# Hybrid attention block on one core: swapping the last two products of the output projection, and spreading the weight sums over a head

## The chip, the cores and the metric

One core of a Trainium2 chip. The metric is the device time of one execution in microseconds, the median of several runs. A profiled execution gives the rows shown below.

## The reference, cut to what matters

512 tokens, width 2048. An input projection gives queries, keys, values and gates for eight stick-breaking heads and latents for eight MLA heads; both attentions give 128 columns a head, which are gated and set side by side as `mixed` (512 x 2048).

```python
mixed = concat([o_a * silu(sb_gate), o_b * silu(mla_gate)], axis=-1)
y = mixed @ w_out                                   # 2048 x 2048
return x + rms_norm(y, post_norm_w)                 # a norm over each row of y
```

The norm needs the sum of squares of a whole row of y before any of the row can be written out.

## The kernel before

Every float32 operand is cut in two parts (`split`: a cast on ScalarE, ACT, gives `hi`; a subtraction on VectorE, DVE, gives `lo`), and each product is three matmuls (`mm3`, L127): hi·hi, hi·lo, lo·hi.

**Order.** A planner writes each engine's instruction list: among instructions whose inputs it reckons ready, the earlier in the program goes first. `tc.keep_in_program_order` pins an instruction behind the one traced just before it on the same engine. All matmuls are pinned, so TensorE (PE) runs in the order of the program; so are SyncE's (SP) loads, the weight sums on DVE (L476) and their loads and stores on GpSimd's (POOL's) DMA queue (L468, L477). Other DVE, ACT and POOL instructions may move. Each engine then runs its list strictly in order.

**Filler.** `filler` yields after each small group of matmuls of the projections; `fill(n)` takes n such steps. The attention heads put them between their own steps, so PE has dense work while DVE and ACT work on a head.

**Stick-breaking heads** (the loop at L924, h = 0 to 7). For each of four query blocks b: scores `z` on PE, mask on DVE (L936), two sigmoids on ACT, a scan on DVE (L940), and the product into `beta` (L942). Then for j = 0 to 3: transposes `tp` on PE, their split `th` (ACT) and `tl` (DVE), and `av` matmuls that read `th` and `tl`.

**Output projection.** `out_group(0)` and `(1)` make y's first 1024 columns directly. The last 1024 columns go by Strassen-Winograd on 2 x 2 blocks, seven products instead of eight (`last_columns`): x = A11·B11; then z = S1·T1, y = S2·T2, v = S3·T3, v += A22·T4, x += A12·B21 and S4·B22. S are sums of blocks of `mixed`, T sums of blocks of w_out. In the code `w11`, `w21`, `w22` are B11, B21, B22. Six products stream their weights (`product`, L563). The weights of the seventh, S4·B22, are loaded and split ahead (`keep_weights`, 16 tiles `woh`, `wol`), so that it can run row block by row block: row block 0 whole, row block 1 in two slices of 256 columns, each in a PSUM bank of its own (`sp`).

`out_piece` (L411) closes a piece of y straight from PSUM: ACT squares and sums it, DVE multiplies by the norm's weight. `sum_piece` (L419) has a sum first: DVE adds a tile, ACT squares, DVE multiplies. `residual` (L618) adds the squares, takes the power on POOL (L625, L626), and multiplies and adds x on DVE (L634), with one piece of the last row block on ACT and POOL (L631, L632).

**Weight sums.** T is made during the stick-breaking heads in eight portions. `load_weight_parts(j)` loads four tiles of 256 KB (`wsum`) on POOL's queue; `weight_sums(j)` makes four DVE subtractions of 128x512, each followed by a store to DRAM (`w_sums`). `w_todo` gives portion j to head j for j = 0 to 6, and portion 7 to head 4 too. The tiles have tag `qrt`, with eight slots; the first four tile pairs of `split_mixed` (L381: load `mx` from DRAM on POOL's queue, split to `mxh`, `mxl`) take `qrt` slots after them. The loads `mx` have tag `mv`, with four slots.

Of the kernel before, what the change touches and what calls it, by code (L numbers as in the profile page):

```python
# [2 lines left out]

# [17 lines left out]
S = 512  # L21
# [3 lines left out]
H = 8  # L25
# [32 lines left out]
def block(ctx: ExitStack, tc: tile.TileContext, a: dict):  # L58
# [16 lines left out]
    def zbank(name, dt=F32):  # L75
        return psum.tile([P, S], dt, tag="z", name=name, bufs=2)
# [10 lines left out]
    def load(out, in_):  # L87
        tc.keep_in_program_order(nc.sync.dma_start(out=out, in_=in_))
# [38 lines left out]
    def mm3(out, sth, stl, mvh, mvl, first, last, **kw):  # L127
        mm(out, sth, mvh, first, False, **kw)
        mm(out, sth, mvl, False, False, **kw)
        mm(out, stl, mvh, False, last, **kw)  # L130
# [280 lines left out]
    def out_piece(b, at, ps, pw, junk=None):  # L411

        w = ps.shape[1]
        square_sum(b, ps, (zbank("junk") if junk is None else junk)[:, :w])
        y = g(f"y{b}", tag=next(y_tags))[:, :w]
        dve.tensor_tensor(out=y, in0=ps, in1=pw, op=ALU.mult)  # L416
        ypw[b][at] = y
# [53 lines left out]
    def weight_sums(j):  # L471

        i, c = j // 2, slice((j % 2) * S, (j % 2 + 1) * S)
        b11, b12, b22, b21 = w_parts.pop(j)
        for n, (out, x, y) in ((0, (b11, b12, b11)), (2, (b12, b22, b12)), (1, (b22, b22, b11)), (3, (b21, b21, b22))):
            tc.keep_in_program_order(dve.tensor_tensor(out=out, in0=x, in1=y, op=ALU.subtract))  # L476
            tc.keep_in_program_order(pool.dma_start(out=w_sums[n][i][:, c], in_=out))  # L477

    def mixed_again(n):
        t = g("mx", tag="mv")  # L480
# [35 lines left out]
    def keep_weights():  # L516

        def loaded(j):
            t = g("wk", tag="mv")
            load(out=t, in_=a["w_o"][3, 4 + j // 2][:, (j % 2) * S:(j % 2 + 1) * S])  # L520
            return t

        raws = [loaded(0), loaded(1)]
        yield
        for j in range(8):
            if j + 2 < 8:
                raws.append(loaded(j + 2))
            hi, lo = g("woh", F32R), g("wol", F32R)
            split(hi, lo, raws.pop(0))
            kept.append((hi, lo))  # L530
            yield
# [3 lines left out]
    def load_x(b0, tag):  # L535

        for b in (b0, b0 + 1):
            x_rows[b] = []
            for i in range(4):
                xr = g("xr", tag=tag)  # L540
                load(out=xr, in_=a["x"][b * P:(b + 1) * P, i * S:(i + 1) * S])
                x_rows[b].append(xr)
                if i % 2:
                    yield
# [18 lines left out]
    def product(banks, which, srcs, start, stop, beside=iter(())):  # L563
        for i in range(4):
            wh, wl = weights(srcs[i], 1024)
            next(beside, None)
            for j in (2 * i, 2 * i + 1):
                s_ = slice((j % 2) * S, (j % 2 + 1) * S)
                for r in range(2):
                    mm3(banks[r], *factor(which, j, r), wh[:, s_], wl[:, s_], start and j == 0, stop and j == 7,  # L570
                        skip_group_check=True)
                    yield

    def last_columns():
        w11, w21 = ([a["w_o"][2, k + i] for i in range(4)] for k in (0, 4))
        x = [bank("sx") for _ in range(2)]
        sums_of = late_sums()
        yield from product(x, "A11", w11, True, False, sums_of)
        s1 = [g("s1", tag="t") for _ in range(2)]
        s15 = [g("s15", tag="t") for _ in range(2)]  # L580
        for r in range(2):
            act.copy(out=s1[r], in_=x[r])
        z = [zbank("sz") for _ in range(2)]
        yield from product(z, "S1", w_sums[0], True, True, sums_of)
        for r in range(2):
            dve.tensor_tensor(out=s15[r], in0=z[r], in1=s1[r], op=ALU.add)
        y = [tbank("sy") for _ in range(2)]
        keeping = keep_weights()
        yield from product(y, "S2", w_sums[1], True, True)
        next(keeping)  # L590
        for r in range(2):
            dve.tensor_tensor(out=s1[r], in0=y[r], in1=s1[r], op=ALU.add)
            dve.tensor_tensor(out=s15[r], in0=y[r], in1=s15[r], op=ALU.add)
        pw2, pw3 = post_weight(2), post_weight(3)
        junk = g("junk", tag="tr")
        v = [bank("sv") for _ in range(2)]
        yield from product(v, "S3", w_sums[2], True, False, keeping)
        for r in range(2):
            sum_piece(2 + r, 3 * S, v[r], s15[r], pw3, junk)
        yield from product(v, "A22", w_sums[3], False, True, both(keeping, load_x(2, "g")))  # L600
        for r in range(2):
            sum_piece(2 + r, 2 * S, v[r], s1[r], pw2, junk)
        yield from product(x, "A12", w21, False, True, load_x(0, "qrt"))
        for r in range(2):
            out_piece(r, 2 * S, x[r], pw2, junk)
        for b in (2, 3):
            residual(b)
        for b in (0, 1):
            cuts = [slice(0, S)] if b == 0 else [slice(0, 256), slice(256, S)]
            for s_ in cuts:  # L610
                ps = zbank("sp")[:, :s_.stop - s_.start]
                for j in range(8):
                    mm3(ps, *factor("S4", j, b), kept[j][0][:, s_], kept[j][1][:, s_], j == 0, j == 7)
                    yield
                sum_piece(b, 3 * S + s_.start, ps, s15[b][:, s_], pw3[:, s_], junk)
            residual(b, b == 1)

    def residual(b, tail=False):  # L618
        xs = x_rows[b]
        n = pieces[b]  # L620
        part = tn("part")
        dve.tensor_reduce(out=part, in_=ssy[b][:, :n - 1], axis=AX.X, op=ALU.add)
        dve.tensor_scalar(out=part, in0=part, scalar1=EPS, scalar2=None, op0=ALU.add)
        r2 = tn("r2")
        pool.tensor_tensor(out=r2, in0=ssy[b][:, n - 1:n], in1=part, op=ALU.add)  # L625
        pool.tensor_tensor(out=r2, in0=r2, in1=mhalf[:, :1], op=ALU.pow)  # L626
        for i, (at, y) in enumerate(sorted(ypw[b].items())):
            w = y.shape[1]
            o = xs[at // S][:, at % S:at % S + w]
            if tail and i == 2:  # L630
                act.activation(out=y, in_=y, func=AF.Copy, scale=r2)  # L631
                pool.tensor_tensor(out=o, in0=y, in1=o, op=ALU.add)  # L632
            else:
                dve.scalar_tensor_tensor(out=o, in0=y, scalar=r2, in1=o, op0=ALU.mult, op1=ALU.add)  # L634
            (nc.sync, nc.scalar)[i % 2].dma_start(out=a["out"][b * P:(b + 1) * P, at:at + w], in_=o)
# [285 lines left out]

    w_todo = [[h] for h in range(H - 1)] + [[]]
    w_todo[H // 2].append(H - 1)
    for h in range(H):  # L924
        kh, kl = need("k", h)
        qh, ql = need("q", h)
        fill(4)
        rows = row_tiles("beta")
        for j in w_todo[h]:
            load_weight_parts(j)  # L930
        for b in range(NB):
            n = (b + 1) * P
            w = max(n, 256)
            z = zbank("z")
            mm3(z[:, :w], tokens(qh, b), tokens(ql, b), kh[:, :w], kl[:, :w], True, True)
            dve.tensor_tensor(out=z[:, n - P:n], in0=z[:, n - P:n], in1=m_sb, op=ALU.add)  # L936
            keep, prod, beta = g("keep", tag="tr"), g("prod", tag="tr"), rows[b]
            act.activation(out=keep[:, :n], in_=z[:, :n], func=AF.Sigmoid, scale=rq_neg[:, b:b + 1])
            act.activation(out=beta, in_=z[:, :n], func=AF.Sigmoid, scale=rq_pos[:, b:b + 1])
            dve.tensor_tensor_scan(out=prod[:, :n][:, ::-1], data0=keep[:, :n][:, ::-1], data1=zero.broadcast_to([P, n]),  # L940
                                   initial=1.0, op0=ALU.mult, op1=ALU.add)
            dve.tensor_tensor(out=beta[:, :n - 1], in0=beta[:, :n - 1], in1=prod[:, 1:n], op=ALU.mult)  # L942
            fill((1, 3, 3, 7)[b])
        for j in w_todo[h]:
            weight_sums(j)
        cur = Weighted(rows, need("v", h // 4), (h % 4) * P)
        for j in range(NB):
            cur.turn(j)
            fill(3)
            cur.add(j)  # L950
        out = cur.finish(need("gate", h))
        if h == H - 1:
            last_mixed[0] = out
        put_aside(h, out)
# [58 lines left out]
```

## Time and profile before

| | |
|---|---|
| median of 3 runs | 852.98 us (851.91 to 856.62) |
| profiled execution, its time | 854.35 us |
| its span, first to last instruction | 852.6 us |
| PE matmul busy | 834.7 us, 98% |
| DVE busy | 484.3 us, 57% |
| ACT busy | 361.7 us, 42% |
| granted TensorE clock, mean | 0.996 |

The profile's rows are times in microseconds from the span's start. PE is busy nearly throughout, so what counts is the few places at which it waits, and the stretch after its last matmul.

### The profile page before, as it was taken

The numbers are of one execution on the slowest core, as the hardware profiler recorded it, in microseconds if no ns is written. First come the engines' busy times: TensorE is split into PE (matmuls) and PEld (weight loads), VectorE is DVE, ScalarE is ACT, GpSimd is POOL, SyncE is SP. The second block draws the span as 40 slices with busy tenths as digits, with TensorE's granted clock in tenths as the row PEclk, the third lists the DMA queues.
The fourth block names the chain that finished last, engine by engine and source line by source line (L and its number), as shares of the span: only waits on it lengthen the run. The fifth ranks groups of instructions, "written<-read, shape, count | busy, mean of one in ns | idle before, by whom it ended". The sixth has DMA issues, their size and how long they took to land.

```text
span 852.6 us, 11037 instructions
## 1 busy us (share of the span) xinstructions
PE 834.7 (98%) x4074; PEld 701.4 (82%) x4074; DVE 484.3 (57%) x869; ACT 361.7 (42%) x622; POOL 90.7 (11%) x189
## 2 busy tenths in 40 slices
PE   8999999999999999999999999999999999999995
PEld 5889988888888888888888888888878887888784
DVE  5576765565665523647374523566473777435875
ACT  6742655545555323334242413333352644334531
POOL 1000000000000020111111020121120121100001
PEclk9999999999999999999999999999999999999998
DMA  9923322222221153434434352345463555526874
GB/s 329 345 81 106 100 81 81 81 93 81 81 88 67 63 185 99 149 107 153 161 124 161 123 200 94 142 145 187 149 210 111 161 196 200 161 98 212 321 282 148
DMA packets 42053, 126.84 MB, mean 149 GB/s; under 512 B 5824, under 2 KB 6352, under 8 KB 42000
## 3 DMA queue, kind: packets, MB, share of 16 engines
q1 hardware_dynamic: 30096, 88.75, 30.0%
q0 software_dynamic: 10608, 35.42, 12.3%
q10 hardware_dynamic: 1296, 1.97, 0.7%
q8 instruction: 32, 0.52, 0.2%
q14 instruction: 21, 0.17, 0.1%
HBM read 109.34 MB, written 16.78 MB: 148 GB/s over the span
## 4 chain that ended last, share of the span: by engine, by line
PE 86%; DVE 4%; DMA 4%; issue 3%; ACT 2%; POOL 1%; SPq 0%; DVEq 0%; POOLq 0%; ACTq 0%
PE gps L122 19%; PE v L122 10%; PE qp L122 10%; PE kp L122 9%; PE y L122 6%; PE cq L122 4%; PE av L122 4%; PE mz L122 3%; DMA mx<-mixed 3%; PE mqp L122 3%; PE sx L122 3%; PE ckv L122 2%; PE tp L125 2%; PE sv L122 2%; PE z L122 2%
## 5 line engine op out<-in xcount | busy, mean ns | idle before, releaser
L99 DVE TENSOR_TENSOR wlo<-raw,whi 128x1024 fp32r<-128x1024 f32 (+2 forms) x137 | 163.3, 1192 | 147.7 <-ACT whi L96 144.1
L96 ACT CAST whi<-raw 128x1024 fp32r<-128x1024 f32 (+2 forms) x137 | 140.4, 1026 | 216.0 <-PE v L122 43.5
L122 PE MATMUL gps<-hh,whi 128*128 128x512 f32 x256 | 102.0, 398 | 0.0
L122 PE MATMUL gps<-hl,whi 128*128 128x512 f32 x256 | 100.1, 391 | 0.0
L122 PE MATMUL gps<-hh,wlo 128*128 128x512 f32 x256 | 99.9, 390 | 0.0
L122 PEld LDWEIGHTS gps<-hh,wlo 128*128 128x128 f32 x256 | 48.0, 188 | 10.6
L99 DVE TENSOR_TENSOR tl<-tp,th 128x512 fp32r<-128x512 f32 (+1 forms) x64 | 31.2, 487 | 42.5 <-ACT th L96 42.0
L96 ACT CAST th<-tp 128x512 fp32r<-128x512 f32 (+1 forms) x64 | 27.2, 424 | 66.2 <-PE tp L125 66.0
L122 PEld LDWEIGHTS gps<-hl,whi 128*128 128x128 f32 x256 | 48.3, 189 | 7.6
L122 PEld LDWEIGHTS gps<-hh,whi 128*128 128x128 f32 x256 | 48.2, 188 | 7.6
L122 PE MATMUL qp<-hh,whi 128*128 128x512 f32 x128 | 52.1, 407 | 0.0
L122 PE MATMUL v<-whi,hh 128*128 128x512 f32 x128 | 50.9, 397 | 0.0
L122 PE MATMUL y<-whi,mxh 128*128 128x512 f32 x128 | 50.3, 393 | 0.4 <-DVE y L416 0.4
L122 PE MATMUL qp<-hh,wlo 128*128 128x512 f32 x128 | 50.1, 391 | 0.0
L122 PE MATMUL qp<-hl,whi 128*128 128x512 f32 x128 | 50.0, 391 | 0.0
L122 PE MATMUL v<-whi,hl 128*128 128x512 f32 x128 | 49.9, 390 | 0.0
L122 PE MATMUL v<-wlo,hh 128*128 128x512 f32 x128 | 49.9, 390 | 0.0
L122 PE MATMUL y<-whi,mxl 128*128 128x512 f32 x128 | 49.9, 390 | 0.0
L122 PE MATMUL y<-wlo,mxh 128*128 128x512 f32 x128 | 49.8, 389 | 0.0
L122 PE MATMUL kp<-hh,whi 128*128 128x512 f32 x128 | 49.8, 389 | 0.0
L122 PE MATMUL kp<-hl,whi 128*128 128x512 f32 x128 | 49.8, 389 | 0.0
L122 PE MATMUL kp<-hh,wlo 128*128 128x512 f32 x128 | 49.8, 389 | 0.0
(290 smaller groups left out, 1798.2 us busy)
## 6 DMA issues: line engine op xcount, KB each, us to landing
raw<-in_w_t SPq DMA_DIRECT2D x64, 512.0 KB, 3.3
raw<-in_w_o SPq DMA_DIRECT2D x24, 512.0 KB, 3.3
mx<-mixed POOLq DMA_DIRECT2D x39, 256.0 KB, 3.4
raw<-in_w_v SPq DMA_DIRECT2D x16, 512.0 KB, 3.2
wsum<-in_w_o POOLq DMA_DIRECT2D x32, 256.0 KB, 5.5
w_sums<-wsum POOLq DMA_DIRECT2D x32, 256.0 KB, 2.7
raw<-w_sums SPq DMA_DIRECT2D x16, 512.0 KB, 3.5
xs<-in_x SPq DMA_DIRECT2D x16, 256.0 KB, 6.2
```

Source lines behind the costliest of these rows:

```text
L96: i = act.copy(out=hi, in_=src)
L99: dve.tensor_tensor(out=lo, in0=src, in1=hi.bitcast(F32), op=ALU.subtract)
L122: tc.keep_in_program_order(pe.matmul(out=out, lhsT=lhsT, rhs=rhs, start=start, stop=stop, **kw))
L125: tc.keep_in_program_order(pe.transpose(out, in_, identity))
```

## The change

1. The last two products change places. S4·B22 streams its weights from `w22` into two banks `z` and is closed by `sum_piece`; A12·B21 goes last, with kept weights, and adds onto x in x's own banks: row block 0 whole, then row block 1 in two column slices of the same bank, each closed by `out_piece`.
2. `weight_sums` becomes a generator: one sum and one store per step. A step is taken behind `beta` of each block b and behind each `av` of j.
3. The parts for head h + 1 are loaded in head h, ahead of `finish`; those for head 0 ahead of the loop.
4. In the last row block, ACT and POOL take the piece of index 4 (columns 1536 to 2047) in place of index 2 (columns 1024 to 1535): with the new slices these are the ones of 512 columns.

```diff
@@ weight_sums
             tc.keep_in_program_order(pool.dma_start(out=w_sums[n][i][:, c], in_=out))
+            yield
@@ keep_weights
-            load(out=t, in_=a["w_o"][3, 4 + j // 2][:, (j % 2) * S:(j % 2 + 1) * S])
+            load(out=t, in_=a["w_o"][2, 4 + j // 2][:, (j % 2) * S:(j % 2 + 1) * S])
@@ last_columns
-        w11, w21 = ([a["w_o"][2, k + i] for i in range(4)] for k in (0, 4))
+        w11, w22 = ([a["w_o"][gi, k + i] for i in range(4)] for gi, k in ((2, 0), (3, 4)))
...
-        yield from product(x, "A12", w21, False, True, load_x(0, "qrt"))
+        z = [zbank("sz") for _ in range(2)]
+        yield from product(z, "S4", w22, True, True, load_x(0, "qrt"))
         for r in range(2):
-            out_piece(r, 2 * S, x[r], pw2, junk)
+            sum_piece(r, 3 * S, z[r], s15[r], pw3, junk)
...
-                ps = zbank("sp")[:, :s_.stop - s_.start]
                 for j in range(8):
-                    mm3(ps, *factor("S4", j, b), kept[j][0][:, s_], kept[j][1][:, s_], j == 0, j == 7)
+                    mm3(x[b][:, s_], *factor("A12", j, b), kept[j][0][:, s_], kept[j][1][:, s_], False, j == 7, skip_group_check=True)
                     yield
-                sum_piece(b, 3 * S + s_.start, ps, s15[b][:, s_], pw3[:, s_], junk)
+                out_piece(b, 2 * S + s_.start, x[b][:, s_], pw2[:, s_], junk)
@@ residual
-            if tail and i == 2:
+            if tail and i == 4:
@@ loop over the stick-breaking heads
+    load_weight_parts(0)
     for h in range(H):
...
-        for j in w_todo[h]:
-            load_weight_parts(j)
+        w_steps = itertools.chain(*(weight_sums(j) for j in w_todo[h]))
         for b in range(NB):
...
+            next(w_steps, None)
             fill((1, 3, 3, 7)[b])
-        for j in w_todo[h]:
-            weight_sums(j)
...
             cur.add(j)
+            next(w_steps, None)
+        if h < H - 1:
+            for j in w_todo[h + 1]:
+                load_weight_parts(j)
         out = cur.finish(need("gate", h))
```

## Rows read from the trace of the kernel before

**Rows 1.** The page's busy times (share of the span, instructions).

```profile
PE 834.7 (98%) x4074; PEld 701.4 (82%) x4074; DVE 484.3 (57%) x869; ACT 361.7 (42%) x622; POOL 90.7 (11%) x189
```

**Rows 2.** Busy time by stretch: us; engines with instructions; clock; DMA share; GB/s.

```profile
401.30:439.10 37.80, 37.80 (x180) 31.62 (x179) 21.08 (x33) 13.35 (x22) 5.29 (x11) 1.00 0.41 146
596.00:633.80 37.80, 36.33 (x170) 29.90 (x170) 22.79 (x37) 16.19 (x27) 8.57 (x17) 1.00 0.50 171
```

**Rows 3.** PE's waits, 600 to 680: waited for, us in total, times, longest.

```profile
PE z L122 <- ACT kh L96: 1.1, 1, 1.1
PE z L122 <- DVE kl L99: 0.3, 1, 0.3
PE av L122 <- DVE tl L99: 0.3, 1, 0.3
```

**Rows 4.** The chain that ended last: start, us, what (`y`: out_group's first matmuls).

```profile
401.32 2.04 PE qp L122 x9
439.10 2.04 PE qp L122 x9
...
595.98 2.04 PE qp L122 x9
...
674.13 2.04 PE y L122 x9
```

**Rows 5.** ACT's timeline: start, us, instruction [idle before, releaser].

```profile
624.23 0.62 ACT L96 CAST mxh<-mx 128x512 fp32r<-128x512 f32 x1 [2.29 <-DMA mx<-mixed]
624.76 0.61 ACT L96 CAST kh<-kr 128x512 fp32r<-128x512 f32 x1
```

**Rows 6.** POOL's timeline around the loads for head 6.

```profile
604.25 0.20 POOL L778 MEMSET tl<- 128x128 f32 x1
...
610.87 0.55 POOL L468 DMA_DIRECT2D wsum<-in_w_o  x1
...
613.62 1.15 POOL L392 DMA_DIRECT2D mx<-mixed  x2
621.39 1.17 POOL L392 DMA_DIRECT2D mx<-mixed  x2 [6.62 <-DVE mxl L99]
```

**Rows 7.** DVE's timeline in an undisturbed head (h = 2).

```profile
431.74 0.68 DVE L476 TENSOR_TENSOR wsum<-wsum 128x512 f32<-128x512 f32 x1
...
439.58 0.69 DVE L942 TENSOR_TENSOR beta<-beta,prod 128x511 f32<-128x511 f32 x1
...
442.52 0.68 DVE L99 TENSOR_TENSOR tl<-tp,th 128x512 fp32r<-128x512 f32 x1
```

**Rows 8.** PE's timeline in the same head.

```profile
440.98 0.60 PE L125 MATMUL tp<-ident,beta 128*128 128x128 f32 x4
...
443.71 0.39 PE L122 MATMUL av<-tl,vh 128*128 128x512 f32 x1
```

**Rows 9.** DVE's timeline at the end.

```profile
834.39 0.69 DVE L416 TENSOR_TENSOR y<-sx,pw 128x512 f32<-128x512 f32 x1 [0.34 <-ACT junk L407]
...
839.79 2.74 DVE L634 SCALAR_TENSOR_TENSOR xr<-y,r,xr 128x512 f32<-128x512 f32 x4 [0.70 <-POOL r L626]
842.45 0.75 DVE L423 TENSOR_TENSOR y<-sp,s 128x256 f32<-128x256 f32 x2
...
845.26 3.21 DVE L634 SCALAR_TENSOR_TENSOR xr<-y,r,xr 128x512 f32<-128x512 f32 x4 [0.70 <-POOL r L626]
```

**Rows 10.** ACT's timeline at the end.

```profile
838.18 0.19 ACT L407 ACTIVATION_READ_ACCUMULATOR junk<-y 128x1 f32 x1
...
843.00 0.42 ACT L407 ACTIVATE junk<-y 128x256 f32<-128x256 f32 x1 [4.63 <-DVE y L423]
843.33 0.18 ACT L407 ACTIVATION_READ_ACCUMULATOR junk<-y 128x1 f32 x1
```

**Rows 11.** PE's timeline: second and last of the 48 matmuls on two slices.

```profile
836.77 0.28 PE L122 MATMUL sp<-wol,s 128*128 128x256 f32 x1
...
842.29 0.28 PE L122 MATMUL sp<-woh,s 128*128 128x256 f32 x1
```

More of the change, by code (lines that the diff above doesn't have):

```diff
@@ L1 @@
+import itertools
 import math
```

## The prediction

> **What bounds the kernel now.** I read the page's busy times first: PE is busy for 834.7 us [rows 1], so the time is the matmuls' own unless PE waits. Then the busy times by stretch, head by head: an undisturbed stick-breaking head has PE busy for all of its 37.80 us, at full clock, while DVE has 21.08 us of work in it. The stretch from 596 to 633.8 is the exception: 36.33 us busy [rows 2]. The list of PE's waits names what it waited for there: 1.1 us for the cast `kh`, 0.3 us for `kl`, 0.3 us for `tl` [rows 3]. What this costs is read better from the chain that ended last, since a busy PE also counts the pipelined ends of its matmuls. From the first `qp` of one head to that of the next it is 439.10 - 401.32 = 37.78 us. The two heads from 595.98 to 674.13 took 78.15 us, and 2 x 37.78 = 75.56: so 2.6 us were lost in head 6 [rows 4].
>
> Why is `kh` late? ACT ran it at 624.76, right behind a cast `mxh` that began at 624.23 after 2.29 us of waiting for the load `mx` [rows 5]. ACT runs in order, so `kh` stood in line behind a cast for the output projection that is needed much later. That load left POOL's queue at 621.39, once an earlier `mxl` had freed a tile; the loads of that pair had left at 613.62, behind the weight parts of head 6, which went from 610.87 on [rows 6].
>
> The other place is the end. After PE's last matmul (842.29 + 0.28 = 842.57 [rows 11]) come add, square, power and the last multiply-adds, which begin at 845.26 [rows 9]. Nothing covers that.
>
> **The change part by part.** *Matmuls.* S4·B22 and A12·B21 have 48 matmuls of 512 columns each when streamed, and as many matmuls and slices when kept as before. SP's loads keep number, size and order; the tiles kept ahead come from another group of w_out. PE's work: 0, hidden by nothing because nothing is added.
>
> *Loads of the weight parts, one head earlier.* The four loads for head 6 are pinned behind POOL's last instruction ahead of them. That was the store of the head's output; now it is the memset of `tl`, at 604.25 against 610.87 for the first load before: some 6.4 us earlier [rows 6]. The pairs `mxh`, `mxl` that take `qrt` slots come after them, and the loads `mx` follow: those of 613.62 and 621.39 should move to about 607 and 615, and the cast that blocked ACT from 624.23 to about 618. Then `kh` has ACT to itself at 624. What is queued behind the moved loads on POOL is the store of the head's output, up to eight issues of 0.55 us [rows 6] later in head 3, four elsewhere; it is read again only by `mx` loads, later on. Gain: between 0 (another cast slips in ahead of `kh`) and 2.6 us. I take 2.6, as the shift is longer than the 2.29 us that ACT waited [rows 5].
>
> *Weight sums between the blocks.* The same 32 subtractions and 32 stores. Before, they were free to run ahead of the scores (one at 431.74 [rows 7]); now each is pinned behind the `beta` of its block. The first three lie in front of later blocks, where DVE pauses while ACT computes sigmoids. The fourth must come after the last `beta` (439.58 + 0.69 = 440.27) and so stands ahead of the split `tl`, which ended at 442.52 + 0.68 = 443.20 [rows 7]. PE reads it at 443.71 [rows 8]: 0.51 us of cover. A sum takes 0.68 us [rows 7], so each head may lose 0.68 - 0.51 = 0.17 us; in seven heads 1.2 us. Below, 0: the planner puts it behind `tl`. Above, the third sum too delays the last chain: 2 x 0.68 - 0.51 = 0.85 us, in seven heads 6.0 us. I take 1.2: if one sum makes the last `beta` late, that is covered, since 440.27 is 0.71 us ahead of the transposes at 440.98 [rows 7, 8]. The second portion's sums of head 4 come behind `av`, where DVE has the 16 us that a head leaves it [rows 2]. A store now waits for its own sum on POOL's queue; behind it there is the memset of the j = 3 transposes, some us later. Nothing.
>
> *The end, without a new wait.* `out_piece` has no add ahead of its square. PE ends at 842.57; the square of 256 columns takes 843.33 + 0.18 - 843.00 = 0.51 us [rows 10]; from a square's end to the first multiply-add it is 839.79 - (838.18 + 0.19) = 1.42 us [rows 9, 10]. So 842.57 + 0.51 + 1.42 = 844.5 in place of 845.26: 0.75 us gained. The multiplication by the norm's weight lies beside the power on POOL.
>
> *The end, with one.* Before, each slice of row block 1 had its bank. Now both lie in one bank of x. The trace shows what happens to two engines on one bank: DVE's multiplication of x, which needs nothing from ACT's square of x, stood 0.34 us idle until that square was done [rows 9]. They only read, and were put one behind the other. If this holds between a matmul and a reader of other columns, the second slice's matmuls must wait for square and multiplication of the first. [...]
>
> The price: a matmul on a slice takes (842.29 - 836.77) / 46 = 0.12 us [rows 11]. The first slice ends at about 839.7, its square at 840.2. Its multiplication then stands on DVE behind the four multiply-adds of row block 0. Those began at 839.79 [rows 9], and without the add (0.7 to 0.8 us) they begin at about 839.0 and end, 2.74 us later [rows 9], at 841.75. Before, the adds of the slices ran at 842.45, behind all four, though the first was ready by 839.8 [rows 9]: the same order is to be expected. Multiplication until 842.15, then 24 x 0.12 = 2.9 us and 0.16 us of drain to 845.2, square to 845.7, and 1.42 us to 847.1. That is 1.85 us later than 845.26. Were the multiplication put ahead of the last multiply-adds, it would be 840.2 + 0.4 + 3.05 + 0.51 + 1.42 = 845.6, 0.3 us later. Range of this term: -0.75 to +1.85. I take 1.85, the case nearest to the rows 9.
>
> *Index 4 in place of 2.* One piece of 512 columns for another, on the same engines: 0.
>
> **Sum:** -2.6 + 1.2 + 1.85 = +0.45 us. The profiled execution took 854.35 us with a span of 852.6; it lies 1.4 us above the median of 852.98, so the sum is put on the median: 853.4 us.
>
> **The rivals.**
> - *No wait at the bank.* Matmuls and readers on other columns of a bank run side by side. For it: columns are apart, and no row shows a matmul held so. Against: the readers in rows 9. -2.6 + 1.2 - 0.75 = -2.15: 850.8 us.
> - *The loss in head 6 stays,* so that the move does not do what it could. The planner may put other `mxh` casts in front of `kh`, for their loads still take turns at four slots. 0 + 1.2 + 1.85 = +3.05: 856.0 us, 0.36% more.
> - *The sums hold the heads up: slower.* Third and fourth sum both lie on the way from the last scores to `tl`: 6.0 us in place of 1.2. For it: each is pinned behind a `beta` and earlier in the program than what follows. Against: DVE idles in this stretch. -2.6 + 6.0 + 1.85 = +5.25: 858.2 us. It passes 0.5% from 0.72 us a head on.
>
> **How the numbers follow.** A measurement of this kernel can tell about 0.5% (4.3 us) from no change. Forecast 0.45, no wait at the bank 0.22, loss stays 0.20, sums hold up 0.10, the rest 0.03. No case reaches 4.3 us of gain: with all three terms at their best it is 2.6 + 0 + 0.75 = 3.35 us, so faster gets 0.06, for what I do not see and for scatter. Slower gets the last rival and the upper edge of the third case, 0.14; the same 0.80. The range from 850.0 to 857.5 takes in the first three cases with about 1 us beyond them, and leaves out the last.
>
> **What would show it.** Head 6 right: its loads `wsum` leave POOL behind the memset near 604, no wait of PE for `kh`, and 75.6 us for the two heads. Sums right: PE waits for `tl` by 0.1 to 0.2 us in each head, DVE with one `wsum` between `beta` and `tl`. The end right: PE idle for some 2.5 us between the slices of row block 1, released by DVE's multiplication. The prediction is wrong if PE waits at transposes in each head, or if its last 48 matmuls run on without a gap.

## The result and the profile after

The changed kernel takes 860.53 us (median of 6, 859.11 to 864.02), the kernel before 852.67 in the same rounds: a ratio of 1.009, interval 1.0064 to 1.0116. It is slower by 0.9%, outside the predicted range, and close to the rival that had a chance of 0.10. The profiled execution has a span of 859.6 us, 7.0 more than before.

Line numbers are now one or two higher: the sums are L477, `beta` L944, `mm3`'s matmuls L123.

PE's waits in the whole span (waited for, us in total, times, longest), to be held against [rows 3]:

```profile
PE av L123 <- DVE tl L100: 3.5, 6, 0.6
PE sx L123 <- DVE y L417: 2.0, 1, 2.0
...
PE tp L126 <- DVE beta L944: 1.1, 1, 1.1
```

Before, `tl` was waited for once; now once in six of the seven heads that take sums (in the seventh, head 3, PE waits 0.9 us for `gt` behind it in the same list). The wait for `kh` is gone. A new wait of 2.0 us stands at the end, for DVE's multiplication of x (L417).

The chain that ended last shows what a head costs (start, us, what; `gps` x15 opens heads 2 and 3):

```profile
427.70 3.40 PE gps L123 x15
...
466.74 3.40 PE gps L123 x15
```

39.04 us a head, where [rows 4] had 37.78: 1.26 us lost in a head that lost nothing before. From the first gate matmul of head 0 to the first `y` matmul of the output projection it is 330.6 us, against 323.5 before: 7.1 us. That is about the difference in the span; the rest nearly cancels (1.0 us more at the end, about as much less at the start and in the output projection together).

Why `tl` is late is on DVE's list. Its timeline in head 2, the head of [rows 7]:

```profile
435.54 0.69 DVE L477 TENSOR_TENSOR wsum<-wsum 128x512 f32<-128x512 f32 x1
436.14 0.29 DVE L938 TENSOR_TENSOR z<-z,m_sb 128x128 f32<-128x128 f32 x1
436.34 1.22 DVE L100 TENSOR_TENSOR wlo<-raw,whi 128x1024 fp32r<-128x1024 f32 x1
437.47 0.95 DVE L942 TENSOR_TENSOR_SCAN prod<-keep,zero 128x384 f32<-128x384 f32 x1
438.53 0.56 DVE L944 TENSOR_TENSOR beta<-beta,prod 128x383 f32<-128x383 f32 x1
439.00 0.69 DVE L477 TENSOR_TENSOR wsum<-wsum 128x512 f32<-128x512 f32 x1
439.60 0.29 DVE L938 TENSOR_TENSOR z<-z,m_sb 128x128 f32<-128x128 f32 x1
440.72 1.23 DVE L942 TENSOR_TENSOR_SCAN prod<-keep,zero 128x512 f32<-128x512 f32 x1 [0.82 <-ACT keep L940]
442.05 0.69 DVE L944 TENSOR_TENSOR beta<-beta,prod 128x511 f32<-128x511 f32 x1
442.65 0.68 DVE L477 TENSOR_TENSOR wsum<-wsum 128x512 f32<-128x512 f32 x1
443.25 0.69 DVE L345 TENSOR_TENSOR gt<-gps,rstd_bc 128x512 f32<-128x512 f32 x1
443.86 1.22 DVE L100 TENSOR_TENSOR wlo<-raw,whi 128x1024 fp32r<-128x1024 f32 x1
444.99 0.69 DVE L348 TENSOR_TENSOR gt<-gt,sg 128x512 f32<-128x512 f32 x1
445.59 0.69 DVE L100 TENSOR_TENSOR tl<-tp,th 128x512 fp32r<-128x512 f32 x1
```

Three sums stand on the way from the scores to `tl`. The second (435.54) pushes the long `wlo` (a subtraction for a projection, 1.22 us) behind the mask of block 2, and the scan waits behind both. The third (439.00) stands in front of the mask of the last block. The fourth (442.65) stands in front of everything that leads to `tl`: two instructions on the gate (`gt`) and another `wlo` come between, and DVE runs them without a pause. PE's timeline shows the last scores and the wait:

```profile
437.00 0.39 PE L123 MATMUL z<-kh,qh 128*128 128x512 f32 x1
...
446.33 0.50 PE L123 MATMUL av<-tl,vh 128*128 128x512 f32 x1 [0.64 <-DVE tl L100]
```

For the same marks in the kernel before, its timelines of PE and then of DVE:

```profile
435.54 0.39 PE L122 MATMUL z<-kh,qh 128*128 128x512 f32 x1
```

```profile
433.47 1.22 DVE L99 TENSOR_TENSOR wlo<-raw,whi 128x1024 fp32r<-128x1024 f32 x1
434.60 0.29 DVE L936 TENSOR_TENSOR z<-z,m_sb 128x128 f32<-128x128 f32 x1
...
437.14 0.29 DVE L936 TENSOR_TENSOR z<-z,m_sb 128x128 f32<-128x128 f32 x1
...
440.19 0.68 DVE L344 TENSOR_TENSOR gt<-gps,rstd_bc 128x512 f32<-128x512 f32 x1
440.79 1.22 DVE L99 TENSOR_TENSOR wlo<-raw,whi 128x1024 fp32r<-128x1024 f32 x1
441.92 0.68 DVE L347 TENSOR_TENSOR gt<-gt,sg 128x512 f32<-128x512 f32 x1
```

From the last scores' first matmul to their mask it was 437.14 - 435.54 = 1.60 us and is 439.60 - 437.00 = 2.60: 1.00 us later. Of this 0.60 is the third sum's (the step from its start to the mask's); the other 0.40 is put down to the second, behind which `wlo` comes later than the mask of block 2 and not ahead of it. The first sum may have a part in the 0.40; no run has the second alone. From the last `beta` to `tl` it was 442.52 - 439.58 = 2.94 [rows 7] and is 445.59 - 442.05 = 3.54: 0.60 more, the fourth. In all `tl` is 1.60 us later; 0.51 of it had cover; 1.09 remains, of the 1.26 us that a head lost. The last 0.17 is not taken apart here.

Head 6 took 40.30 us by PE's timeline, 2.5 more than 37.78: the sums' 1.26, and about as much again for another reason. ACT's timeline:

```profile
625.16 1.25 ACT L97 CAST mxh<-mx 128x512 fp32r<-128x512 f32 x2 [2.33 <-DMA mx<-mixed]
...
628.14 0.61 ACT L97 CAST kh<-kr 128x512 fp32r<-128x512 f32 x1
...
640.38 0.62 ACT L97 CAST mxh<-mx 128x512 fp32r<-128x512 f32 x1 [3.13 <-DMA w_sums<-wsum]
640.91 0.69 ACT L940 ACTIVATE keep<-z,rq_neg 128x512 f32<-128x512 f32 x1
```

`kh` now runs on time, as the loads' earlier start was to bring about. But another `mxh` waits 3.13 us for the store of a weight sum to land, since it takes that sum's `qrt` slot. The sigmoid of the last block, `keep`, stands behind it, and PE waits 1.1 us for `beta`. That the store comes late, as its sum does, is not all of it. The run with spread sums and the old order of products (spread alone, below) has the same store at the same place, and there head 6 lost no more than the others. POOL's issue of the store and ACT's cast in the changed kernel and then in that run:

```profile
636.19 0.55 POOL L478 DMA_DIRECT2D w_sums<-wsum  x1 [2.03 <-DVE z L938]
```

```profile
636.01 0.55 POOL L478 DMA_DIRECT2D w_sums<-wsum  x1 [2.02 <-DVE z L938]
```

```profile
638.50 0.62 ACT L97 CAST mxh<-mx 128x512 fp32r<-128x512 f32 x1 [1.43 <-DMA w_sums<-wsum]
```

From the issue to the cast it is 640.38 - 636.19 = 4.19 us in the one execution and 2.49 in the other. So with the sums spread a cast on ACT, and `keep` behind it, depends on when a store lands. Why this one landed later is not shown, nor whether it does so in every execution.

The end, as PE's and then DVE's timeline have it:

```profile
837.26 0.39 PE L123 MATMUL sx<-woh,mxh 128*128 128x512 f32 x1
...
845.46 0.28 PE L123 MATMUL sx<-woh,mxl 128*128 128x256 f32 x1
847.70 0.39 PE L123 MATMUL sx<-woh,mxh 128*128 128x256 f32 x1 [1.96 <-DVE y L417]
```

```profile
844.57 2.74 DVE L636 SCALAR_TENSOR_TENSOR xr<-y,r,xr 128x512 f32<-128x512 f32 x4 [0.19 <-POOL r L628]
847.23 0.42 DVE L417 TENSOR_TENSOR y<-sx,pw 128x256 f32<-128x256 f32 x1
...
852.26 3.21 DVE L636 SCALAR_TENSOR_TENSOR xr<-y,r,xr 128x512 f32<-128x512 f32 x4 [0.47 <-POOL r L628]
```

The second slice's matmuls wait until DVE has multiplied the first, and that stands behind the four multiply-adds of row block 0, as forecast. From the first matmul of row block 0 (837.26; before, the line below from PE's timeline) to the end of the span it was 852.6 - 831.22 = 21.4 us and is 859.6 - 837.26 = 22.3.

```profile
831.22 0.39 PE L122 MATMUL sp<-woh,s 128*128 128x512 f32 x1
```

### The profile page after: what moved, and what is told of

It is laid out like the page before. It is cut to its first block, busy times and chain, and to the rows that moved or that the text cites. A ratio compares the mean times of both kernels' runs of the same rounds, so it can differ in the third digit from the quotient of the medians.

```text
span 859.6 us, 11031 instructions
## 1 busy us (share of the span) xinstructions
PE 837.9 (97%) x4074; PEld 701.5 (82%) x4074; DVE 486.4 (57%) x868; ACT 360.7 (42%) x622; POOL 90.2 (10%) x189
## 3 DMA queue, kind: packets, MB, share of 16 engines
q10 hardware_dynamic: 1296, 1.97, 0.7%
## 4 chain that ended last, share of the span: by engine, by line
PE 81%; DVE 10%; DMA 3%; ACT 3%; issue 2%; SPq 0%; POOL 0%; DVEq 0%; ACTq 0%; POOLq 0%
PE gps L123 14%; PE y L123 10%; PE kp L123 10%; PE v L123 10%; PE qp L123 7%; PE cq L123 4%; PE av L123 4%; PE mz L123 3%; PE mqp L123 3%; PE sz L123 3%; DVE prod L942 2%; PE sx L123 2%; PE ckv L123 2%; DVE wlo L100 2%; DVE wsum L477 2%
## 5 line engine op out<-in xcount | busy, mean ns | idle before, releaser
L123 PE MATMUL gps<-hh,whi 128*128 128x512 f32 x256 | 102.1, 399 | 0.0
L123 PE MATMUL gps<-hl,whi 128*128 128x512 f32 x256 | 100.2, 391 | 0.0
L123 PE MATMUL gps<-hh,wlo 128*128 128x512 f32 x256 | 100.0, 391 | 0.0
L123 PEld LDWEIGHTS gps<-hh,wlo 128*128 128x128 f32 x256 | 48.1, 188 | 10.6
L123 PEld LDWEIGHTS gps<-hl,whi 128*128 128x128 f32 x256 | 48.3, 189 | 7.6
L123 PEld LDWEIGHTS gps<-hh,whi 128*128 128x128 f32 x256 | 48.2, 188 | 7.6
L123 PE MATMUL qp<-hh,whi 128*128 128x512 f32 x128 | 52.1, 407 | 0.0
L123 PE MATMUL v<-whi,hh 128*128 128x512 f32 x128 | 50.9, 398 | 0.9 <-DVE gt L345 0.9
L123 PE MATMUL y<-whi,mxh 128*128 128x512 f32 x128 | 50.2, 393 | 0.0
L123 PE MATMUL qp<-hh,wlo 128*128 128x512 f32 x128 | 50.1, 392 | 0.0
L123 PE MATMUL qp<-hl,whi 128*128 128x512 f32 x128 | 50.1, 391 | 0.0
L123 PE MATMUL v<-whi,hl 128*128 128x512 f32 x128 | 50.0, 390 | 0.0
L123 PE MATMUL v<-wlo,hh 128*128 128x512 f32 x128 | 49.9, 390 | 0.0
L123 PE MATMUL y<-whi,mxl 128*128 128x512 f32 x128 | 49.9, 390 | 0.0
L123 PE MATMUL kp<-hh,whi 128*128 128x512 f32 x128 | 49.9, 390 | 0.0
L123 PE MATMUL y<-wlo,mxh 128*128 128x512 f32 x128 | 49.9, 390 | 0.0
L123 PE MATMUL kp<-hl,whi 128*128 128x512 f32 x128 | 49.9, 390 | 0.0
L123 PE MATMUL kp<-hh,wlo 128*128 128x512 f32 x128 | 49.8, 389 | 0.0
```

Of the source, the lines that this page charges most:

```text
L123: tc.keep_in_program_order(pe.matmul(out=out, lhsT=lhsT, rhs=rhs, start=start, stop=stop, **kw))
```

## The experiments

Theory S: the sums that stand in each head's chain on DVE cost the time. Theory B: the wait at x's bank is the large term, as the prediction had it. Rival L: the earlier loads of the weight parts do the harm. The first four kernels take the change apart; they ran on one chip with the kernel before.

**Swap alone.** The kernel before with this edit only (the closing pieces as in the change):

```diff
-        yield from product(x, "A12", w21, False, True, load_x(0, "qrt"))
+        yield from product(z, "S4", w22, True, True, load_x(0, "qrt"))
```

> The kernel before with the two last products swapped, and nothing else: weight sums and their loads stand where they stood. Theory S (the 7 us come from the sums that stand in each head's chain on DVE): only the end differs, 1.0 us later by the two profiles (row block 0's first matmul to the end of the span was 21.4 us before and 22.3 after), so 853.7 us. Theory B (the wait at x's bank is the large term, as the prediction had it): 1.9 us or more over before, 854.5 us. Rival L (the earlier loads of the weight parts do the harm): as S here.

855.52 us, ratio 1.002 (1.0009 to 1.0032): by the ratio 1.7 us over before, between 0.8 and 2.7. Theory S had 1.0; theory B 1.9 or more: this run alone doesn't tell them apart, but it leaves most of the loss to the other parts. The profiled execution was the slowest of its runs, 858.04 us. Head 6 keeps the wait for `kh`, 1.6 us in this execution. The pause between the slices is 1.97 us long, and the slice behind it was slow: busy time by stretch of this run, of the last 24 matmuls (us; PE, PEld, DVE, ACT, POOL; clock; DMA share; GB/s):

```profile
843.20:847.50 4.30, 4.27 (x24) 3.97 (x24) 0.19 (x2) 0.00 (x0) 0.00 (x0) 0.68 0.39 115
```

and the same stretch of the changed kernel:

```profile
847.60:850.90 3.30, 3.13 (x24) 2.93 (x24) 0.27 (x3) 0.03 (x1) 0.00 (x0) 1.00 0.53 161
```

The same 24 matmuls took 4.27 us at a mean granted clock of 0.68, and 3.13 at 1.00. By PE's timeline those of swap alone start 0.12 us apart up to 844.76 and 0.21 apart from 844.95 on. So a pause of the same length was followed by another 1.1 us of loss in one profiled execution and by none in the other.

**Spread alone.** The changed kernel with the products in the old order:

```diff
-        yield from product(z, "S4", w22, True, True, load_x(0, "qrt"))
+        yield from product(x, "A12", w21, False, True, load_x(0, "qrt"))
```

> The changed kernel with the two products back in the old order: sums between the blocks, loads early. Theory S: the heads lose what they lose in the changed kernel, 6 to 7 us over before, 859 us, with a wait for tl in each of seven heads. Theory B: 0 to 1 us over before. Rival L: as S.

859.58 us, ratio 1.007 (1.0055 to 1.0084): theory S. PE waits for `tl` six times, 3.5 us in the list of waits, as in the changed kernel. Nearly all of the loss is there without the swap, so theory B as the main cause falls.

**Early loads alone.**

```diff
-            next(w_steps, None)
             fill((1, 3, 3, 7)[b])
+        for _ in w_steps:
+            pass
...
             cur.add(j)
-            next(w_steps, None)
```

and the products in the old order.

> The kernel before with the weight parts loaded one head earlier, and nothing else: the sums run at once behind the four blocks, as before. Theory S: no wait for tl in any head; if the earlier loads also clear ACT for kh in head 6, as the prediction had it, its 2.6 us go and the time is 850 us, if not, it is before's 852.7. Rival L: 6 us over before, 859 us.

850.78 us, ratio 0.9969 (0.9958 to 0.9979): 2.6 us faster than before, and rival L falls. All waits of PE from 340 us on, and then heads 6 and 7 in the chain:

```profile
PE sv L123 <- DVE y L424: 0.4, 1, 0.4
```

```profile
622.33 3.40 PE gps L123 x15
...
660.11 3.40 PE gps L123 x15
```

Head 6 takes 37.78 us like the others. ACT's timeline shows why: the last `mxh` in front of `kh` is done in time.

```profile
619.38 1.25 ACT L97 CAST mxh<-mx 128x512 fp32r<-128x512 f32 x2 [1.58 <-DMA mx<-mixed]
623.10 0.61 ACT L97 CAST kh<-kr 128x512 fp32r<-128x512 f32 x1
```

**Swap and early loads,** the sums at once:

```diff
-            next(w_steps, None)
             fill((1, 3, 3, 7)[b])
+        for _ in w_steps:
+            pass
...
             cur.add(j)
-            next(w_steps, None)
```

> The changed kernel with the four sums at once behind the blocks again: swap and early loads stay. Theory S: the end's 1.0 us, less what the early loads give in head 6 (0 to 2.6 us): 851 to 853.7 us. Theory B: 854.5 us. Rival L: 860 us, as the changed kernel.

852.68 us, ratio 0.9984 (0.9974 to 0.9994), within what theory S gave; rival L falls here too. Its last slice also ran partly at a lower clock: a mean of 0.64 over the 24 matmuls, which took 4.60 us.

Between the two marks (first gate matmul of head 0, first `y` matmul) the profiles give the cost of each part without the end:

| kernel | us between the marks |
|---|---|
| before | 323.5 |
| changed | 330.6 |
| swap alone | 324.9 |
| spread alone (loads early) | 329.4 |
| early loads alone | 320.8 |
| swap and early loads | 320.9 |

The marks of spread alone and then of early loads alone, by PE's timelines:

```profile
349.57 0.39 PE L123 MATMUL gps<-hh,whi 128*128 128x512 f32 x1
...
678.93 0.39 PE L123 MATMUL y<-whi,mxh 128*128 128x512 f32 x1
```

```profile
351.96 0.39 PE L123 MATMUL gps<-hh,whi 128*128 128x512 f32 x1
...
672.80 0.39 PE L123 MATMUL y<-whi,mxh 128*128 128x512 f32 x1
```

The spread costs 329.36 - 320.84 = 8.5 us, or 9.7 with the swap; the 1.2 us between these two is the store in head 6 that landed late. The early loads give 323.46 (673.97 - 350.51, the same marks before) - 320.84 = 2.6. So the 7.1 us of the changed kernel are 8.5 + 1.2 - 2.6.

The next four ask which sums count, and what PE waits for between the slices.

**The fourth sum behind `av`.** Spread sums, products in the old order:

```diff
-            next(w_steps, None)
+            if b < 3:
+                next(w_steps, None)
...
+        for _ in w_steps:
+            pass
         if h < H - 1:
```

> The run of the spread sums with the old order of products (859.6 us), with the fourth sum of each portion moved from behind the last beta to behind the first av. Theory S, in the sizes of the changed kernel's trace: tl comes 1.6 us late in a head, of which the second sum gives 0.4, the third 0.6 and the fourth 0.6, and a head loses 1.25 us. Without the fourth tl is 1.0 us late, a head loses about 0.6, seven heads 4.5 us in place of 8.7: 855.3 us. Rival F (only the sum right in front of tl counts, as the prediction had it): no loss is left, the 850.8 us of the early loads alone. Rival P (any pinned sum in a head's chain costs all of it): 859.6 us.

855.22 us, ratio 1.0025 (1.0016 to 1.0035); 325.4 us between the marks, 4.6 over the early loads alone. That is theory S in size; rival F and rival P fall. PE's waits for `tl` are shorter:

```profile
PE av L123 <- DVE tl L100: 1.2, 4, 0.3
```

**Third and fourth behind `av`.** The same with `if b < 2`.

> As the run before, with the third and fourth sum moved behind the first av's. Theory S: tl is 0.4 us late, inside its cover of 0.5 us, and no head loses anything: 850.8 us, as with the early loads alone. Rival F: the same. Rival P: 859.6 us or, in proportion to two sums of four, 855 us.

851.36 us, ratio 0.9978 (0.9965 to 0.9992); 321.3 us between the marks. No wait for `tl` is left in the list. Over all heads two sums a head between the blocks cost about 0.4 us, three 4.6, four 8.5.

**Slices in banks of their own.** Swap and early loads, sums at once; x gets three banks, and A11·B11's second row block is made in two slices:

```diff
-        x = [bank("sx") for _ in range(2)]
+        x = [bank("sx") for _ in range(3)]
...
+                    if r == 1 and len(banks) == 3:
+                        for i in range(2):
+                            q_ = slice(s_.start + i * 256, s_.start + (i + 1) * 256)
+                            mm3(banks[1 + i][:, :256], *factor(which, j, r), wh[:, q_], wl[:, q_], start and j == 0, stop and j == 7,
+                                skip_group_check=True)
...
-        v = [bank("sv") for _ in range(2)]
+        v = [zbank("sv") for _ in range(2)]
...
-        z = [zbank("sz") for _ in range(2)]
+        z = [tbank("sz4") for _ in range(2)]
...
+                xb = x[0] if b == 0 else x[1 + s_.start // 256][:, :256]
...
-                    mm3(x[b][:, s_], *factor("A12", j, b), kept[j][0][:, s_], kept[j][1][:, s_], False, j == 7, skip_group_check=True)
+                    mm3(xb, *factor("A12", j, b), kept[j][0][:, s_], kept[j][1][:, s_], False, j == 7, skip_group_check=True)
```

> The run with swap and early loads (852.7 us), with the two column slices of x's second row block in two banks of their own from A11.B11 on, so that the last slice's matmuls share no bank with the readers of the first; A11.B11 then has 48 matmuls of 256 columns in place of 24 of 512, 0.3 us more. Theory B2 (the pause of 2.0 us between the slices is the shared tile and bank): the pause goes, 2.1 - 0.3 = 1.8 us less, 850.9 us. Rival Q (PE waits there for something else that DVE does late): the pause stays, 853.0 us.

849.76 us, ratio 0.9964 (0.9949 to 0.998). The pause is gone, so it came from what the slices shared; rival Q falls. They shared a bank and, in the program, one tile; the run parts both at once and doesn't say which of the two made the wait. Row block 0 begins at 827.66 and the last multiply-adds (L648 in this kernel) at 840.51, 12.85 us later, where before it was 845.26 - 831.22 = 14.04 (PE's and DVE's timelines):

```profile
827.66 0.39 PE L123 MATMUL sx<-woh,mxh 128*128 128x512 f32 x1
```

```profile
840.51 3.21 DVE L648 SCALAR_TENSOR_TENSOR xr<-y,r,xr 128x512 f32<-128x512 f32 x4 [0.47 <-DMA out<-xr]
```

**The row block whole.** Swap and early loads, sums at once:

```diff
-            cuts = [slice(0, S)] if b == 0 else [slice(0, 256), slice(256, S)]
+            cuts = [slice(0, S)]
...
-            if tail and i == 4:
+            if tail and i == 3:
```

> The run with swap and early loads (852.7 us), with the second row block of A12.B21 done in one piece of 512 columns, like the first. Theory B2: no pause of 2.1 us, 0.3 us less of matmuls (24 x 0.227 in place of 48 x 0.12), 0.2 us more of square: 850.5 us. Rival Q: the pause moves in front of the row block or to its end, 852.7 us. Rival T (what the slices hide at the end is worth more than the pause): 853 us or more.

850.03 us, ratio 0.9962 (0.995 to 0.9974): theory B2 again, and rival T falls: slices on one bank and a row block in one piece differ by the pause, and slices on two banks are no faster than the one piece, as far as the intervals tell.

The last two ask whether the pin behind `beta` is the fault, and whether the changed kernel is mended by it.

**Sums not pinned.** Spread sums, products in the old order:

```diff
-            tc.keep_in_program_order(dve.tensor_tensor(out=out, in0=x, in1=y, op=ALU.subtract))
+            dve.tensor_tensor(out=out, in0=x, in1=y, op=ALU.subtract)
```

> The run of the spread sums with the old order of products (859.6 us), same places in the program, but the sums not pinned behind the beta that was traced before them: the planner may move each to where it reckons DVE free. Theory S: the harm lies in the place on DVE's list alone, and the planner moves the sums off the way from the scores to tl (behind the splits tl, into the next projections): no loss in any head, 850.8 us as with the early loads alone. Rival R (the harm lies in the stores or loads that go with each sum): 855 to 859 us.

852.52 us, ratio 0.999 (0.998 to 0.9999): 1.7 us over the forecast of theory S, but 7 below the pinned sums, so rival R falls. In head 2 DVE's timeline now has no sum from 426.00 to the first `tl` at 442.43. The heads take 37.78 us again, all but head 6 (39.65 by PE's timeline): there the planner's new order left part of the old loss, as PE's waits show.

```profile
PE z L123 <- DVE kl L100: 0.7, 1, 0.7
PE z L123 <- ACT kh L97: 0.6, 1, 0.6
```

**Both repairs in the changed kernel:** the edit just shown, and the three banks.

> The changed kernel with two repairs: the sums not pinned, and the second row block's slices of x in banks of their own. Theory S with B2: no loss in the heads, none between the slices, early loads' gain kept: 849.8 us, as the early loads with swap and own banks. If either repair fails beside the other: 851 us with the pause, 858 us with the sums in the way.

852.48 us, ratio 0.9984 (0.9973 to 0.9995), against 1.009 unmended, though 2.7 us above the forecast. It has the same loss in head 6 (322.6 us between the marks, 1.7 over the early loads alone) and a wait of 1.0 us of the second `out_group` for DVE. That this wait belongs to DVE's order there is likely and was not tried.

The fastest are early loads with the swap, with the slices in own banks (0.9964) or the row block whole (0.9962). Early loads alone stand at 0.9969. These intervals overlap, so what the swap adds to the early loads stays open; by the profiles the own banks gain 1.1 us from row block 0 to the end (20.24 us, against 21.35 with early loads alone) and give back 0.5 us in A11·B11 (11.36 us to the next product's first matmul, against 10.88, by PE's timelines).

## Why the prediction was wrong

**Matmuls, loads, index 4.** Right: 4074 matmuls in both profiles, and nothing in the waits points to them.

**Early loads.** Right, in size too: 2.6 us forecast, 2.6 measured with the loads alone, by way of `kh` on ACT. In the changed kernel it did not show in head 6's length: the wait for `kh` was gone, but the sums and the store that landed late took as much there.

**Sums between the blocks.** This is the step that failed: "The first three lie in front of later blocks, where DVE pauses while ACT computes sigmoids." They did not fit. The term was put at 1.2 us and measured 8.5 (spread with early loads against early loads alone). The cover of 0.51 us was read rightly, and so was the fourth sum's 0.6. But the third sum took its full 0.6 us in front of the last mask, and 0.4 more came from the sums before it, with `wlo` (1.22 us) now behind the mask of block 2, so that the next scan was late. The sentence that hid this is "if one sum makes the last `beta` late, that is covered": its 0.71 us were read at the transposes alone. But `tl` hangs on the last `beta` by a second way, DVE's own list, where `gt`, `wlo` and `gt` follow `beta` without a pause, and there the cover is 0.51 us for all the sums together. Its own sign of being right, a wait for `tl` of 0.1 to 0.2 us a head, came out at 0.6. Even the bound of 6.0 us was too low, as it counted the third and the fourth alone. The evidence named against the rival, that DVE idles in this stretch, was true of the sum of its idle time. But its last pause, 0.82 us, stands between mask and scan, and the third sum stood in front of that mask, where nothing took it up.

The stores were put at nothing, too. Their issues, 0.54 us each on POOL's queue, gave PE no wait (its list names POOL nowhere in the changed kernel), but a cast `mxh` that takes a sum's slot waits for the store to land: about 1.2 us in head 6 of the profiled execution. With the 1.0 us of the end, and 1.1 less at the start and in the output projection, which no term of the sum has and nothing here explains, -2.6 + 8.5 + 1.2 + 1.0 - 1.1 make the 7.0 us of the span.

**Rivals.** The slower rival named the right mechanism and the right place and forecast 858.2 us; the measured 860.5 lies beyond it. Its chance of 0.10 was the mistake: the reason that it gave itself, that each sum is pinned behind a `beta` and earlier in the program than what follows, already put each sum in front of the next step of the chain.

**The end.** Right in mechanism: the wait at the bank came, and behind the four multiply-adds. The size was off: forecast 1.85 us; from row block 0's first matmul to the last multiply-adds the changed kernel takes 852.26 - 837.26 = 15.00 us, against 14.04 before: 0.96. What was mis-sized is the way from a square to the first multiply-add, 1.42 us in the forecast, and it counts twice. The last square's end at 851.34 (ACT's timeline) leaves 852.26 - 851.34 = 0.92 us, and row block 0's at 843.66 leaves 844.57 - 843.66 = 0.91, so the multiply-adds in front of the wait were earlier too:

```profile
843.46 0.20 ACT L408 ACTIVATION_READ_ACCUMULATOR junk<-sx 128x1 f32 x1
...
851.15 0.19 ACT L408 ACTIVATION_READ_ACCUMULATOR junk<-sx 128x1 f32 x1
```

The difference is POOL's first addition, 0.69 us at 838.45 in the kernel before and 0.19 at 843.73 and 851.42 here. Where the clock fell (a mean of 0.68 over the last slice), the end cost more: 856.3 - 832.79 = 23.5 us from row block 0's first matmul (PE's timeline) to the end of the span with the swap alone.

That a matmul would wait for a reader of other columns was the author's estimate: no row of the kernel before shows it. What they have is two readers of one bank, DVE's standing 0.34 us idle until ACT's was done [rows 9]. The runs show 1.96 us of pause (changed kernel) and 1.97 (swap alone, swap and early loads) with the slices on one bank and tile, and none with banks of their own.

## What to carry to other kernels

Work that DVE has time for on average (busy for 57% of the span here) can still cost its full length, less what cover there is, when it stands in the list between two steps of a chain that another engine waits for: here the third and the fourth sum made `tl` 0.60 us later each, against 0.51 us of cover for all. Count the cover at each such step, from the wait that ends last, and add up every instruction put in front of it, with what it displaces. Put such work behind the chain's last step (with the fourth sum there the loss was 4.6 us in place of 8.5, with the third too about 0.4), or where no step of the chain is ready. And two column slices of one PSUM bank, in one tile, did not overlap one's reading with the other's matmuls here (1.96 us of pause, none in two banks): plan a bank of its own, from its first matmul on, for a slice that is to be closed early, or leave the row block whole.

## What the runs showed of the hardware

Behind a pause of PE of 1.97 us the granted clock was lower in the profiles of two kernels (swap alone, swap and early loads: means of 0.68 and 0.64 over the next 24 matmuls), and behind one of 1.96 us in the changed kernel it stayed at 1.00. Without this pause it was 1.00 in the kernel before from 831.30 to 842.00 us; and in four more (early loads alone, third and fourth behind `av`, own banks, row block whole) the matmuls of row block 1 start 0.12 us apart on 256 columns and 0.23 apart on 512, to the last one. One execution of each kernel was profiled, so the runs show a lower clock behind two of three such pauses and don't say when it comes. The same first addition on POOL in `residual` took 0.69 us in some places and 0.19 to 0.24 in others; the rows don't show why.
